# Two layers of a streaming encoder on one core: a modulation split throughout, later rows normed early, a last gate beside the first output tile, and norm steps, loads and weight splits placed elsewhere

## The chip, the cores and the metric

The kernel runs on one core of a Trainium2 chip, in one launch. A core has a matrix engine (TensorE, PE in the profile), VectorE (DVE), ScalarE (ACT), GpSimd (POOL) and the sync engine (SP), each with its own queue of instructions. The metric is the device time of one execution in microseconds (us); less is better.

## The reference, cut to what matters

Two layers run over 2048 prompt rows and 32 sample rows of width 1024. Layer 0 mixes with a gated linear recurrence (RG-LRU), layer 1 with forgetting attention (FoX). All is fp32.

```python
def _adaln(c, w, b):
    mod = jax.nn.silu(c) @ w + b                 # [., 3072], w is [1024, 3072]
    shift, scale, gate = jnp.split(mod[:, None, :], 3, axis=-1)

def layer(i, x, c):
    sh, sc, gt = _adaln(c, ada_w[i], ada_b[i])
    h = _rmsnorm(x, norm_pre[i]) * (1.0 + sc) + sh
    y = _rglru_branch(h, ...) if i == 0 else _fox_branch(h, ...)
    return x + gt * _rmsnorm(y, norm_post[i])

def _rglru_branch(h, ...):                       # width 1536, 12 blocks of 128
    xb, gate = jnp.split(h @ w_in, 2, axis=-1)
    xc = conv_b + sum(xp[:, k:k + T] * conv_w[k] for k in range(4))
    r, ig = sigmoid(xblk @ w_a + b_a), sigmoid(xblk @ w_x + b_x)
    log_a = -8 * r * softplus(-lam)
    a, u = exp(log_a), sqrt(-expm1(2 * log_a)) * (ig * xc)
    hs = scan of hs[t] = a[t] * hs[t-1] + u[t]
    return (hs * silu(gate)) @ w_out

def _fox_branch(h, ...):                         # 16 heads of 64, 512 cached rows
    q, k, v, g, fl = jnp.split(h @ w_in, ...)
    log_f = log_sigmoid(fl + b_f); cum = cumsum(log_f)
    p = softmax(q k / 8 + cum[q] - cum[k], causal)
    return ((p @ v) * silu(g)) @ w_out
```

## The kernel before

Every fp32 product is made of three fp32r matmuls: each operand is split into a high part (a copy rounded to fp32r on ScalarE or GpSimd, `hi_act` L95, `hi_pool` L98) and a low part (the difference, `lo_dve` L104 on VectorE), and hi×hi, hi×lo and lo×hi are accumulated. An instruction scheduler fixes the order on each engine at build time, from the order in which the generators below are advanced and from the pools' buffers: `get(role)` takes a buffer of a pool (h 32, w 5, raw 3, half 5, ahalf 11, c 12, wg 2) and waits for its last user. All DMAs go through the one queue of SP, in the order in which they are issued. Tile names in the profile are the pools' names, and PSUM banks are called pj, st, mx, pva and pvb.

The stages, in order of time:

- The modulation of layer 0. `ada(layer, ns, ...)` loads the 512-wide columns n of `ada_w` as 8 tiles each (L243), multiplies them (L296, 34 rows) and finishes (L258 to L276) into `shv`, `gsv` (shift and scaled norm weight) or, for n ≥ 4, the gate, stored to `gp_d`. A tile for which `whole(i)` holds is multiplied unsplit in fp32; of the first call's 32 tiles that is every third one. Beside it, `prenorm` loads the rows of x in four groups of 256 (L337), takes mean squares on ScalarE (`stats`, L346), scales on VectorE (L353), transposes on PE (L372) and applies scale and shift (L378).
- The RG-LRU blocks, twice 12 (`lru_in`, half 0 and 1): chains of 24 matmuls (L556) for x and gate, `conv`, the block before's `gates` (L569, two sigmoids L570) and `tail` (L589 to L612: Exp, Tanh, products, Sqrt, scan, store of z). The list `before` holds the gates and the tail of the block before, which are called behind the first chunk and behind `conv`. As fillers run: the rest of the modulations of both layers, x's second half, the k and v cache.
- The output tiles of layer 0: `out_tiles` makes 16 tiles of 128 rows and one of the 32 sample rows, 72 matmuls each (L725, 12 steps k of 6), with z of the next tile loaded and split half way. `end` applies the gate and the residual (L753, L754). Then `norm_tile` norms the new rows for layer 1 in steps, one behind each k of the next tile: squares, mean and power, scaling (L445), transposes and affine (L452, L453) in two steps, hi, lo and store to `hb_d`. The last gate of layer 1, `last = ada(1, (4, 5), ...)`, all unsplit, is advanced once per three k.
- Layer 1: `proj` (L962 for v, L1001 for q, k and g) for two halves of the rows, with the normed rows read back by `load_h`, merged by `merge` with the `attention` stream. That stream takes key blocks step by step: row maxima (L1147, L1150), scores (L1181, L1185), exponentials (L1187), lows (L104), products with v (L1233, L1234). Where a job isn't ready it yields None, and the projection goes on. Behind the projection come the split of w3 (`load_wout`), 7 output tiles inside the attention stream (`out_tiles`, 48 matmuls each) and 10 behind it.

`merge` alternates by credit: each advance of the projection gives the attention stream its cost in ns times 1.25, and a None sets the credit to 0.

```python
            if k == 0 and end is not None:
                nxt = end()
```

## Time and profile before

| | |
|---|---|
| median of three runs | 3038.46 us (3029.72 to 3040.52) |
| the profiled execution: its time, its span | 3031.66 us, 3029.7 us |
| mean granted clock of PE | 0.985 |
| PE busy | 2869.4 us, 95% of the span |
| VectorE, ScalarE, GpSimd busy | 61%, 48%, 41% |
| matmul instructions | 14948 |

Times in the profile are counted from the span's start. A busy share says little of what a stage is worth; the waits of PE and the tables by stretch say where time can go. The span and the time of the profiled execution differ by 2 us, which lie around the program.

### The profile page before, as it was taken

The numbers are of one execution on the slowest core, as the hardware profiler recorded it, in microseconds if no ns is written. First come the engines' busy times: TensorE is split into PE (matmuls) and PEld (weight loads), VectorE is DVE, ScalarE is ACT, GpSimd is POOL, SyncE is SP. The second block draws the span as 40 slices with busy tenths as digits, with TensorE's granted clock in tenths as the row PEclk, the third lists the DMA queues.
The fourth block names the chain that finished last, engine by engine and source line by source line (L and its number), as shares of the span: only waits on it lengthen the run. The fifth ranks groups of instructions, "written<-read, shape, count | busy, mean of one in ns | idle before, by whom it ended". The sixth has DMA issues, their size and how long they took to land.

```text
span 3029.7 us, 45098 instructions
## 1 busy us (share of the span) xinstructions
PE 2869.4 (95%) x14948; PEld 2293.8 (76%) x14948; DVE 1837.2 (61%) x3282; ACT 1465.3 (48%) x2962; POOL 1255.6 (41%) x1166
## 2 busy tenths in 40 slices
PE   6999999999999989999999999999999999989998
PEld 3777788897666677777777677887888788766776
DVE  7688777777432335646554565766776676676622
ACT  4565544556333333535354443665566556555621
POOL 5445443333222232434343332554555545455632
PEclk9999999999999999999999999999999999998999
DMA  7565675443644587676776776556555556464243
GB/s 277 197 220 199 218 270 192 151 152 127 191 135 129 161 302 254 187 247 187 222 220 210 227 222 192 147 176 154 152 155 152 165 148 176 131 164 121 82 135 96
DMA packets 407002, 548.40 MB, mean 181 GB/s; under 512 B 77096, under 2 KB 241064, under 8 KB 406768
## 3 DMA queue, kind: packets, MB, share of 16 engines
q1 hardware_dynamic: 406768, 545.50, 59.1%
q8 instruction: 119, 1.95, 0.3%
q14 instruction: 115, 0.94, 0.1%
HBM read 333.13 MB, written 212.22 MB: 180 GB/s over the span
## 4 chain that ended last, share of the span: by engine, by line
PE 38%; DMA 8%; DVE 6%; issue 5%; POOL 4%; ACT 3%; SPq 1%; POOLq 0%; DVEq 0%; ACTq 0%
PE pj L1001 13%; PE pj L962 4%; PE mx L1147 4%; PE st L1185 3%; PE st L1181 3%; PE pva L1233 3%; PE pvb L1234 3%; DVE ahalf L104 2%; DMA rc<-dn_d 1%; POOL ahalf L1210 1%; DVE mxs L1150 1%; PE pj L725 1%; DMA ahalf<-q_d 1%; POOL half L754 1%; PE mx L1376 1%
## 5 line engine op out<-in xcount | busy, mean ns | idle before, releaser
L1210 POOL TENSOR_TENSOR ahalf<-ahalf,ahalf 128x512 f32<-128x512 f32 (+2 forms) x528 | 582.5, 1103 | 418.7 <-ACT ahalf L1187 405.1
L1001 PE MATMUL pj<-h,w 128*128 128x512 f32 (+1 forms) x2304 | 585.3, 364 | 1.2 <-DVE half L104 1.2
L1187 ACT ACTIVATE ahalf<-st 128x512 fp32r<-128x512 f32 (+3 forms) x640 | 341.3, 533 | 376.0 <-PE st L1185 327.7
L104 DVE TENSOR_TENSOR ahalf<-st,ahalf 128x512 fp32r<-128x512 f32 (+3 forms) x640 | 386.9, 606 | 206.9 <-ACT st L1188 192.7
L1001 PEld LDWEIGHTS pj<-h,w 128*128 128x128 f32 x2304 | 424.5, 191 | 83.9 <-DVE half L104 1.4
L1150 DVE TENSOR_REDUCE mxs<-mx 128x1 f32<-128x512 f32 (+3 forms) x640 | 372.2, 605 | 148.0 <-PE mx L1147 84.9
L1188 ACT ACTIVATE st<-st 128x512 f32<-128x512 f32 (+3 forms) x640 | 339.8, 531 | 0.0
L1181 PE MATMUL st<-ahalf,kv 128*128 128x512 f32 (+3 forms) x640 | 244.0, 381 | 24.0 <-DVE ahalf L104 17.0
L1233 PE MATMUL pva<-ahalf,vs 128*128 128x512 f32 (+3 forms) x640 | 240.9, 388 | 10.8 <-POOL ahalf L1200 6.6
L962 PE MATMUL pj<-w,h 128*128 128x256 f32 (+3 forms) x1296 | 234.3, 288 | 12.1 <-DVE flog L977 5.4
L1185 PE MATMUL st<-ahalf,kb 96*128 96x512 f32 (+3 forms) x640 | 242.6, 386 | 1.0 <-ACT ahalf L1168 0.6
L1234 PE MATMUL pvb<-ahalf,vs 128*65 128x512 f32 (+3 forms) x640 | 228.1, 366 | 5.7 <-DVE od L1262 3.5
L1147 PE MATMUL mx<-kb,qm 96*128 96x512 f32 (+3 forms) x640 | 225.4, 384 | 7.2 <-DMA ext_d<-half 6.1
L556 PE MATMUL pj<-h,w 128*128 128x512 f32 (+1 forms) x1032 | 226.0, 369 | 0.8 <-POOL h L98 0.7
L962 PEld LDWEIGHTS pj<-w,h 128*128 128x128 f32 (+1 forms) x1296 | 192.3, 187 | 24.7 <-issue 7.5
L556 PEld LDWEIGHTS pj<-h,w 128*128 128x128 f32 x1032 | 177.3, 192 | 32.6 <-POOL h L98 0.9
L104 DVE TENSOR_TENSOR ahalf<-ahalf,ahalf 128x512 fp32r<-128x512 f32 (+2 forms) x183 | 143.9, 788 | 92.6 <-ACT ahalf L95 59.1
L104 DVE TENSOR_TENSOR w<-raw,w 128x1024 fp32r<-128x1024 f32 (+3 forms) x85 | 104.7, 1232 | 150.1 <-ACT w L95 68.5
L1001 PE MATMUL pj<-h,raw 128*128 128x272 f32 (+1 forms) x576 | 188.5, 327 | 0.0
L98 POOL TENSOR_SCALAR w<-raw 128x1024 fp32r<-128x1024 f32 (+3 forms) x68 | 76.1, 1120 | 251.5 <-DMA raw<-in_wqkg 54.2
L725 PE MATMUL pj<-h,ahalf 128*128 128x512 f32 (+1 forms) x408 | 168.2, 413 | 10.4 <-DVE ahalf L104 5.4
L1181 PEld LDWEIGHTS st<-ahalf,kv 128*128 128x128 f32 x640 | 121.7, 190 | 69.2 <-DVE ahalf L104 37.8
(325 smaller groups left out, 5615.5 us busy)
## 6 DMA issues: line engine op xcount, KB each, us to landing
wp_d<-w SPq DMA_DIRECT2D x60, 512.0 KB
vs<-v_d SPq DMA_DIRECT2D x96, 256.0 KB
kv<-k_d SPq DMA_DIRECT2D x192, 128.0 KB
ahalf<-q_d SPq DMA_DIRECT2D x192, 128.0 KB
raw<-in_w SPq DMA_DIRECT2D x44, 512.0 KB
ahalf<-in_ada_w SPq DMA_DIRECT2D x64, 256.0 KB
hb_d<-wg SPq DMA_DIRECT2D x32, 512.0 KB
v_d<-half SPq DMA_DIRECT2D x64, 256.0 KB
```

Of the source, the lines that this page charges most:

```text
L104: dve.tensor_tensor(o, i, f(h), ALU.subtract)
L556: pe.matmul(ps[:, :b - a], l, cols(r, a, b), start=i == 0, stop=i == 23)
L962: pe.matmul(ps[:m, :nw], l, r, start=c == 0, stop=c == 23)
L1001: pe.matmul(ps[:, :b - a], l, cols(r, a, b), start=c == 0, stop=c == 23)
L1147: pe.matmul(ps[:sw, :kw], u.qm[0:96, s0:s0 + sw], kb, start=True, stop=not last)
L1150: dve.tensor_reduce(u.mxs[:sw, si, c:c + 1], ps[:sw, :kw], axis=AX.X, op=ALU.max)
L1181: pe.matmul(ps[:kw, c0:nq], j.ka[k0 // 512][:, kc:kc + kw], u.qa[:, c0:nq], start=True, stop=False)
L1185: pe.matmul(ps[:kw, c0:nq], j.kb[k0 // HALF][0:96, kd:kd + kw], u.qb[0:96, c0:nq], start=False, stop=True)
L1187: act.activation(ph[:kw, c0:nq], ps[:kw, c0:nq], AF.Exp, scale=0.125)
L1188: act.activation(ps[:kw, c0:nq], ps[:kw, c0:nq], AF.Exp, scale=0.125)
L1210: pool.tensor_tensor(u.acc[:kw, c0:nq], f(ph)[:kw, c0:nq], u.acc[:kw, c0:nq], ALU.add)
L1233: pe.matmul(u.pva[:, c:nq], vs[:kw, 0:128], ph[:kw, c:nq], start=ti == 0, stop=last)
```

## The change

Nine edits, independent of each other in the code:

1. The first modulation splits all its 32 tiles; the high parts alternate between ScalarE and GpSimd. Its bias tiles move from the pool c to the pool half.
2. `prenorm` loads the groups 2 and 3 into the pool c as soon as their turn comes before the first block, takes their statistics ahead of group 1's transposes, and `lru_in` gets `fill`: while the first two chains run, it advances the norm by one step behind every three matmuls.
3. The LRU's `tail` is cut in two: Exp, Tanh and products run behind the last chunk's x chain, Sqrt, scan and store behind `conv`.
4. The last gate's tiles go into the pool w, `out_tiles` is started ahead of the last block's gates (z of tile 0 loaded and split), and the modulation advances behind every k.
5. `norm_tile` has two more empty steps ahead of its transposes.
6. `load_h` for the second 512 columns moves from the last tile's loop into the 16 V steps.
7. `LOAD_STEPS` is 18, was 10.
8. q is loaded six steps ahead of a unit's end, was four.
9. w3's raw tiles are loaded two ahead, and its split is handed out in pieces that cost 1500 ns of credit each.

```diff
-ADA_FIRST, ADA_LAST = 8, 6
+ADA_FIRST, ADA_LAST = 8, 5
-LOAD_STEPS = 10
+LOAD_STEPS = 18
...
-                    hi_pool(a, t)
+                    (hi_act if ahead > 6 and i % 2 else hi_pool)(a, t)
...
-                    x = get("xn", [w, pw])
+                    x = get("xn" if gi < 2 else "any", [w, pw])
...
-        ahead = 2
-        for gi in range(ahead):
+        for gi in range(2):
             load(gi)
-        done = 0
+        for gi in range(2):
+            stats(gi)
+        yield 0.0
+        for gi in range(2, len(groups)):
+            load(gi)
+        yield 0.0
         for gi, (t0, n, w) in enumerate(groups):
-            while done < min(gi + (1 if gi == 1 else 2), len(groups)):
-                stats(done)
-                done += 1
-            yield 0.0
+            if gi == 1:
+                stats(2)
+                stats(3)
...
         del o2
         yield
+        yield
+        yield
         for k0 in (0, 4):
...
+                if fill is not None:
+                    next(fill, None)
...
             dve.scalar_tensor_tensor(th, r, 1.0, th, ALU.add, ALU.mult)
+            s.update(a=a, th=th)
+
+        def tail2(n):
+            s = st.pop(n)
+            r, ig, sg, a, th = s["r"], s["ig"], s["sg"], s["a"], s["th"]
             act.activation(th, th, AF.Sqrt)
...
+                if ci == len(chs) - 1:
+                    before[1]()
                 ps = bank()
                 chain(ps, wgh, wgl, a, b)
...
             conv(n)
-            before[1]()
-            before = (lambda n=n: gates(n), lambda n=n: tail(n))
+            before[2]()
+            before = (lambda n=n: gates(n), lambda n=n: tail(n), lambda n=n: tail2(n))
...
                     (hi_pool if k % 2 else hi_act)(a, t[:, c])
+                    if ahead:
+                        yield 1500.0
                     lo_dve(b, t[:, c], a)
...
-            yield 0.0
+            del t, a, b, prs
+            if ahead:
+                load(k + ahead)
+            yield 1500.0 if ahead else 0.0
...
-            lds = [(max(0, late - 4), lambda: q_load(u))]
+            lds = [(max(0, late - 6), lambda: q_load(u))]
...
-        set_roles(first, "c", N_C, "any", "gp", "wout", "ap", "ab")
+        set_roles(first, "c", N_C, "any", "gp", "wout", "ap")
+        set_roles(big, "half", N_HALF, "ab")
...
-        run(ada(0, (0, 2, 1, 3), bank0, bank0, ADA_FIRST, lambda i: i % 3 == 0))
+        run(ada(0, (0, 2, 1, 3), bank0, bank0, ADA_FIRST))
...
-        blocks = lru_in(0, h, bank0, bank1, lc, rest)
+        blocks = lru_in(0, h, bank0, bank1, lc, rest, pre)
...
+        set_roles(big, "w", N_W, "aw")
+        gps = {0: None, 1: None}
+        tiles = list(range(8)) + [16] + list(range(8, 16))
+        out = out_tiles(tiles, NB, z_d, io["x"], x1_d, gps, bank0, w, post=lambda t, o2: norm_tile(t, o2, bank1))
+        next(out)
         last = ada(1, (4, 5), bpvb, bank0, ADA_LAST, lambda i: True)
-        next(last)
...
         for i in range(16 * NB):
             next(out)
-            if i % 3 == 0:
-                next(last, None)
+            next(last, None)
...
             if k < KD:
-                for g in range(2):
-                    run(load_h(h, hb_d, g, 512 * g, 512, [k]))
+                run(load_h(h, hb_d, 0, 0, 512, [k]))
         tail = run(out)
+        loads = load_h(h, hb_d, 1, 512, 512)
...
             next(tail, None)
+            next(loads, None)
         run(tail)
+        run(loads)
...
-        yield from load_wout(io["w3"], NP, w)
+        yield from load_wout(io["w3"], NP, w, 2)
```

Of what this does to the order on PE, three places follow. The first is the passage from the last RG-LRU chain to the output tiles, before the change: the last split modulation step (`scs`), then tile 0 (L725), the last gate's unsplit steps (`scf`, L296) and the last block's gates (L569).

```order
L296 MATMUL pvb_6118<-ahalf_6629,scs 34x512
L296 MATMUL pvb_6118<-ahalf_6630,scs 34x512
L725 MATMUL pj_7001<-h_6637,ahalf_6983 128x512
L725 MATMUL pj_7001<-h_6638,ahalf_6983 128x512
L296 MATMUL pvb_6845<-ahalf_6831,scf 34x512
L569 MATMUL pva_6889<-c_6791,half_6280 128x354
L569 MATMUL mx_6894<-c_6791,half_6280 128x354
L569 MATMUL mx_6899<-c_6791,half_6280 128x354
L296 MATMUL pvb_6845<-ahalf_6833,scf 34x512
L569 MATMUL pva_6889<-c_6792,half_6280 128x354
```

After the change (L754 is the tile's line, L574 the gates'):

```order
L754 MATMUL pj_7036<-h_6736,ahalf_6888 128x512
L754 MATMUL st_7037<-h_6738,ahalf_6888 128x512
L754 MATMUL pj_7036<-h_6735,ahalf_6889 128x512
L754 MATMUL st_7037<-h_6737,ahalf_6889 128x512
L296 MATMUL pvb_7060<-w_7054,scf 34x512
L574 MATMUL pva_6942<-c_6866,half_6345 128x354
L574 MATMUL mx_6947<-c_6866,half_6345 128x354
L574 MATMUL mx_6952<-c_6866,half_6345 128x354
L754 MATMUL pj_7036<-h_6902,ahalf_6892 128x512
L754 MATMUL st_7037<-h_6904,ahalf_6892 128x512
L574 MATMUL pva_6942<-c_6867,half_6345 128x354
```

Ahead of these rows stand the first three steps k of tile 0, each with a modulation step behind it: PE now finds 24 matmuls of the tile and four modulation steps ahead of the gates, where two matmuls and one step stood.

The second place is the third output tile, around the first transpose (L452) of the norm of the tile before; the weights h_66.. and h_68.. change with each step k of six matmuls. Before:

```order
L296 MATMUL pvb_7251<-ahalf_7249,scf 34x512
L725 MATMUL pj_7430<-h_6849,ahalf_7367 128x512
L725 MATMUL st_7431<-h_6851,ahalf_7367 128x512
L725 MATMUL pj_7430<-h_6850,ahalf_7367 128x512
L725 MATMUL st_7431<-h_6852,ahalf_7367 128x512
L725 MATMUL pj_7430<-h_6849,ahalf_7368 128x512
L725 MATMUL st_7431<-h_6851,ahalf_7368 128x512
L452 MATMUL mx_7481<-ident,c_7454 128x128
L725 MATMUL pj_7430<-h_6859,ahalf_7367 128x512
```

After (the transpose is L455):

```order
L754 MATMUL pj_7495<-h_6912,ahalf_7417 128x512
L754 MATMUL st_7496<-h_6914,ahalf_7417 128x512
L754 MATMUL pj_7495<-h_6922,ahalf_7416 128x512
L754 MATMUL st_7496<-h_6924,ahalf_7416 128x512
L754 MATMUL pj_7495<-h_6923,ahalf_7416 128x512
L754 MATMUL st_7496<-h_6925,ahalf_7416 128x512
L754 MATMUL pj_7495<-h_6922,ahalf_7417 128x512
L754 MATMUL st_7496<-h_6924,ahalf_7417 128x512
L455 MATMUL mx_7570<-ident,c_7518 128x128
L754 MATMUL pj_7495<-h_6932,ahalf_7416 128x512
```

The transpose moved from behind the fifth step k, 30 matmuls, to behind the seventh, 42; it is so in each tile from the third on.

The third place is where the second projection ends (L1001) and the attention steps go on (L1147 maxima, L1181 and L1185 scores, L1233 and L1234 products). Before, up to the first output tile of layer 1 (L725):

```order
L1181 MATMUL st_28503<-ahalf_28105,kv_27789 128x512
L1185 MATMUL st_28503<-ahalf_28106,kb_9698 128x512
L1234 MATMUL pvb_28294<-ahalf_28362,vs_9702 65x512
L1147 MATMUL mx_28510<-kb_9698,qm_9701 128x512
L1147 MATMUL mx_28513<-kb_9698,qm_9701 128x512
L1233 MATMUL pva_28293<-ahalf_28506,vs_9702 128x512
L1181 MATMUL st_28534<-ahalf_28105,kv_28064 128x512
L1185 MATMUL st_28534<-ahalf_28106,kb_9698 128x512
L1234 MATMUL pvb_28294<-ahalf_28389,vs_9702 65x512
L1343 MATMUL mx_28518<-identr,mx_s 32x32
L1147 MATMUL mx_28541<-kb_9699,qm_9701 128x512
L725 MATMUL pj_28491<-h_28403,w_28485 128x512
```

After, from the same attention step on (L1176 maxima, L1210 and L1214 scores, L1262 and L1263 products), no tile has begun:

```order
L1210 MATMUL st_28474<-ahalf_28122,kv_27844 128x512
L1214 MATMUL st_28474<-ahalf_28123,kb_9753 128x512
L1263 MATMUL pvb_28352<-ahalf_28422,vs_9757 65x512
L1176 MATMUL mx_28481<-kb_9753,qm_9756 128x512
L1176 MATMUL mx_28484<-kb_9753,qm_9756 128x512
L1262 MATMUL pva_28351<-ahalf_28448,vs_9757 128x512
L1372 MATMUL mx_28491<-identr,mx_s 32x32
L1176 MATMUL mx_28503<-kb_9754,qm_9756 128x512
L1176 MATMUL mx_28506<-kb_9754,qm_9756 128x512
L1178 MATMUL mx_28506<-mask_q,identr 128x128
```

The first matmul of an output tile moved from 25 rows behind the projection's last one to 122 rows behind it, from the third attention step behind the projection to the sixteenth. Before attention's last step stand 216 of the 816 matmuls of these tiles before the change and 90 after it.

## Rows read from the trace of the kernel before

**Rows 1.** The page: span; busy time of each engine.

```profile
span 3029.7 us, 45098 instructions
...
PE 2869.4 (95%) x14948; PEld 2293.8 (76%) x14948; DVE 1837.2 (61%) x3282; ACT 1465.3 (48%) x2962; POOL 1255.6 (41%) x1166
```

**Rows 2.** Windows: stretch, length, busy us per engine, clock, DMA share, GB/s.

```profile
0.00:56.00 56.00, 34.55 (x110) 11.62 (x110) 43.10 (x103) 17.07 (x38) 32.20 (x49) 0.92 0.78 269
80.00:729.00 649.00, 635.46 (x3338) 538.30 (x3337) 488.99 (x580) 346.24 (x493) 259.99 (x199) 0.99 0.58 195
729.00:776.00 47.00, 34.24 (x117) 20.43 (x116) 38.14 (x48) 25.54 (x33) 16.36 (x9) 0.82 0.49 155
776.00:1096.00 320.00, 303.93 (x1300) 214.64 (x1299) 101.73 (x197) 121.81 (x304) 78.40 (x83) 1.00 0.54 165
1096.00:1130.00 34.00, 28.11 (x201) 26.45 (x200) 8.74 (x24) 10.53 (x30) 12.85 (x26) 0.95 0.96 314
1820.00:1832.00 12.00, 5.89 (x47) 5.48 (x46) 3.63 (x7) 1.00 (x2) 0.00 (x0) 0.85 0.80 229
1832.00:2660.00 828.00, 807.79 (x4727) 674.71 (x4727) 553.96 (x1121) 472.68 (x1039) 415.40 (x366) 0.99 0.57 157
2660.00:2690.00 30.00, 24.34 (x116) 19.13 (x115) 20.59 (x35) 16.58 (x31) 16.53 (x14) 0.94 0.62 186
2690.00:2875.00 185.00, 172.61 (x799) 129.60 (x798) 132.71 (x253) 108.58 (x233) 108.55 (x98) 0.94 0.42 116
```

**Rows 3.** Windows, matmuls of L725 alone (output tiles): PE, PEld.

```profile
2880.00:3029.00 149.00, 137.13 (x593) 107.16 (x591) 0.99 0.38 116
```

**Rows 4.** Waits of PE, whole span: us in total, times, longest.

```profile
PE mx L452 <- DVE c L445: 9.3, 9, 1.2
...
PE pva L452 <- DVE c L445: 6.3, 6, 1.3
PE mx L1147 <- DMA ext_d<-half: 6.1, 1, 6.1
PE pj L725 <- DVE ahalf L104: 5.4, 1, 5.4
PE pj L962 <- DVE flog L977: 5.4, 3, 4.8
PE pj L725 <- ACT ahalf L95: 5.0, 2, 3.8
PE st L1181 <- DMA ahalf<-q_d: 4.6, 5, 1.9
PE pvb L296 <- DVE half L259: 3.7, 2, 2.3
```

**Rows 5.** Timeline of DVE: start, length, instruction; idle before it.

```profile
44.30 1.52 DVE L104 TENSOR_TENSOR c<-h,c 128x512 fp32r<-128x512 f32 x1
...
756.04 2.20 DVE L104 TENSOR_TENSOR c<-raw,c 128x1024 fp32r<-128x1024 f32 x1 [5.24 <-ACT c L95]
...
765.74 1.21 DVE L104 TENSOR_TENSOR c<-raw,c 128x1024 fp32r<-128x1024 f32 x1
```

**Rows 6.** Windows, matmuls of L296 alone (modulation): PE, PEld.

```profile
729.00:776.00 47.00, 9.33 (x16) 1.48 (x16) 0.82 0.49 155
```

**Rows 7.** Groups by line from 0 to 57 us: busy, mean ns, idle before.

```profile
L104 DVE TENSOR_TENSOR c<-h,c 128x512 fp32r<-128x512 f32 x21 | 18.7, 925 | 1.8 <-POOL c L98 1.8
```

**Rows 8.** Timeline of PE, the third chain's first matmul.

```profile
75.57 0.50 PE L556 MATMUL pj<-h,w 128*128 128x512 f32 x1 [0.70 <-POOL h L98]
```

**Rows 9.** Groups by line from 80 to 729 us: table loads ahead of Sqrt.

```profile
L594 ACT ACT_TABLE_LOAD x22 | 28.2, 1283 | 0.4
```

**Rows 10.** Waits of PE from 2660 to 2690 us.

```profile
PE st L1181 <- DVE ahalf L104: 5.6, 3, 3.2
```

**Rows 11.** Windows of 12 us, columns as in the second group.

```profile
2736.00:2748.00 12.00, 8.29 (x29) 4.61 (x29) 7.83 (x15) 7.05 (x15) 9.55 (x10) 0.94 0.56 167
2784.00:2796.00 12.00, 12.00 (x48) 9.28 (x48) 5.65 (x13) 6.21 (x16) 5.35 (x6) 0.57 0.40 121
```

More of the change, by code (lines that the diff above doesn't have):

```diff
@@ L383, in prenorm @@
                 yield 110 * n
-            if gi + ahead < len(groups):
-                load(gi + ahead)
             flags.add(("n", layer, half, gi))
@@ L656, in lru_in, with load_wout, load @@
             conv(n)
-            before[1]()
-            before = (lambda n=n: gates(n), lambda n=n: tail(n))
-        return before
-    def load_wout(src, kn, w):
+            before[2]()
+            before = (lambda n=n: gates(n), lambda n=n: tail(n), lambda n=n: tail2(n))
+        return before
+    def load_wout(src, kn, w, ahead=0):
+        raw = {}
+        def load(k):
+            if k < kn:
+                raw[k] = get("raw", [128, D])
+                sp.dma_start(raw[k], src[128 * k:128 * k + 128, :])
+        for k in range(ahead):
+            load(k)
         for k in range(kn):
-            t = get("raw", [128, D])
-            sp.dma_start(t, src[128 * k:128 * k + 128, :])
+            if not ahead:
+                load(k)
+            t = raw.pop(k)
             if k >= 8:
@@ L1658, in hybrid_kernel @@
         run(wout)
[L1659 removed]
+        gps.update({i: load_gp(0, i) for i in range(2)})
         ones_rows()
         h = new_h()
[L1662 to L1663 removed]
         for i in range(16 * NB):
             next(out)
[L1666 to L1667 removed]
+            next(last, None)
         run(last)
```

18 lines of the change are left out of this document (9 added, 9 removed).

## The prediction

> **What bounds the kernel now.** I read the page first: TensorE (PE) is busy in 2869.4 of 3029.7 us, the next engine, VectorE (DVE), in 61% of the span [rows 1]. So only two things can shorten the run much: idle time of PE, 160 us in all (3029.7 − 2869.4), and stretches at a clock under 1.00, where a busy PE does less. The second view is a table of stretches [rows 2]; the reader is to see in it that the idle time is not even. The matmul stages are almost full (80 to 729 us: 13.5 idle of 649). Idle are the start (21.5 of 56), the passage from the RG-LRU blocks to the output tiles (729 to 776: 12.8 of 47, at a clock of 0.82), the tiles (776 to 1096: 16.1 of 320), the passage to the attention layer (1096 to 1130: 5.9), 6.1 of 12 at 1820, and the end of attention (2660 to 2875: 18.1 at 0.94). Third, the waits of each such stretch say what ended them. As a yardstick I take the pitch of the output tiles' matmuls where nothing interrupts them: 137.13 us for 593, or 0.231 us each [rows 3].
>
> **The change part by part.** The sum is made against the profiled execution, 3031.66 us for a span of 3029.7.
>
> Norm steps further apart. PE waits 15 times for the DVE scaling of L445 that its transposes read, 9.3 + 6.3 = 15.6 us, each at most 1.3 [rows 4]: nearly all that is idle in the tiles' stretch. The order moves the transposes of a tile from behind 30 of its 72 matmuls to behind 42. Those 12 matmuls take 12 × 0.231 = 2.8 us, more than twice the longest wait, and the instructions that the transposes wait for stay where they are. What is late next is the tile's evacuation, split and store, 2.8 us later in a 20 us tile (320/16), which nobody awaits before the tile is over. I take −14; at the least −8, if the evacuations now meet the next tile's split of z on ScalarE; at the most −15.6.
>
> The last gate beside the first output tile. Now tile 0 ends at about 776 us, 46 us after the last chain, and its own work is 72 × 0.231 = 16.7. In that stretch PE waits 5.4 us for the low part of z, 5.0 for the high one and up to 2.3 for a gate's finish [rows 4]. After, z of tile 0 is loaded and split ahead of the last gates, PE has the tile's first four steps and four modulation steps to do before the gates, and all 16 steps of the modulation stand in the first two tiles, where 7 did in the first. The limit is then the w2 rows with k ≥ 8: their low parts stand on DVE at 756.0 to 767 [rows 5], among the products and scan of the last block. Tile 0 needs the last of them for its last step, so it ends about 768.5 if DVE keeps its times, and about 763 if the z splits that left that stretch pull it forward. That is 7 to 12 us, and PE will have done some 5 more modulation steps by then, of 9.33/8 = 1.2 us each (seven whole steps and a split one stand in that stretch [rows 6]). The ceiling is all idle time and the clock's loss, 12.8 + 0.18 × 34.24 = 19. I take −13; bounds −4 (only the z waits that the gates don't hide) and −19.
>
> More load steps. At 1820 us PE waits 6.1 us for the bias rows ext_d [rows 4]. The attention stream now lets the projection make 18 steps instead of 10 before it computes its first maxima. A step is three matmuls, so eight are 8 × 3 × 0.231 = 5.5 us of PE work in place of the wait: −5.5; bounds 0 (the work is only moved within a stretch that is full anyway) and −7 (the clock of 0.85 there recovers as well). q loads two steps earlier are for the waits on q_d, 4.6 us in five [rows 4]; they hold slots of the ahalf pool longer, so −1, between +3 and −4.6.
>
> The later h loads in the 16 V steps. They move behind the last tile's stores on the SP queue, so that the V tiles 4 and 5 wait for DMA, and the last tile's transposes come later. The stretch holds 5.9 us of idle time now, 5.4 of it waits for flog, which stay [rows 2, 4]. I take +1, between −4 and +5.
>
> First modulation all split, prenorm early. Eleven weight tiles lose their fp32 matmuls and gain split ones, which PE has room for; DVE gets 11 more lows of 0.925 us by the mean [rows 7], 10 us. The last low starts at 44.30 and ends at 45.8 [rows 5], late in the 56 us before the first chain, so these are not free; but DVE stood idle 12.9 of the first 56 us [rows 2], and some of the lows fall there. The biases move to a pool whose slots are free only after the rates of the LRU, so the weight loads behind the fourth queue behind a bias load that waits for DVE, and there the awaited instruction stands behind the low of the first weight tile: a tile has to land and be split, its low alone 0.925 us, before the fifth is fetched. That is 2 to 4 us of loads lost, an estimate of mine, ahead of a chain whose last low is late by DVE's queue and not by its load. Against it the later rows' transposes leave the gap between the second and third chain, where the last wait of PE is 0.70 us [rows 8]. I take +1; bounds −4 (DVE's waits go and the idle 12.9 us absorb all) and +8 (most of the 10 us on the path).
>
> The LRU tail in two parts. Ten more table loads of 1.28 us [rows 9] are 13 us on ScalarE, which is busy 346 of 649 us in that stage [rows 2]; PE fills it, so 0 (±4).
>
> Split of w3 spread out, tiles later. After the projection ends, attention has 78 steps left in either order. Before, 216 of the output tiles' 816 matmuls stand among them, after, 90; 126 × 0.231 = 29 us move behind attention's end. Whether that is lost depends on how far attention alone shrinks. The 185 us from 2690 hold 81 steps, 210 tile matmuls and 172.61 us of busy PE, so a step's own PE work is (172.61 − 210 × 0.231)/81 = 1.53 us, and a step takes 2.28 [rows 2, 3]. DVE, the next, has 132.71/81 = 1.64 with its share of the tiles. With 90 tile matmuls inside, PE has 81 × 1.53 + 21 = 145 us of work; at the same busy share of 93% that is 156, plus 29 behind is 185: no change. And the bunched waits of 2660 to 2690 (5.6 us [rows 10]) may go, but the splits now fall among steps with less cover. The granted clock of these 185 us is 0.94 now, with one fall to 0.57 over 12 us at 2784, not long after 3.7 us of 12 were idle at 2736 [rows 11]; by the mean the price above stands, and by the fall it is rival 2. The Trainium skill (TensorE: Matmul & The Clock Gate, "A second HAM failure mode: psum-queue depth-cycling") tells of a kernel whose PE idled briefly between groups of matmuls so often that its clock went to and fro; by that rule attention without filler loses its clock, as rival 2 has it, and the sum would go by that rival's price. I take 0. Bounds: −16 (145 + 29 against 185, and the 5.6), and +29 (the pace of 2.28 stays, and the removed work only bares waits).
>
> Sum: −14 − 13 − 5.5 − 1 + 1 + 1 + 0 + 0 = −31.5, so 3031.66 − 31.5 = 3000. The profiled execution lies 6.8 us under the median 3038.46 of the runs shown, and near their lowest, 3029.72; against the median the sum gives 3007. I keep 3000.
>
> **Rivals.**
> 1. Attention alone keeps its pace: +29 in the last part, 3029. For it: between 2690 and 2875 PE waits for DVE, ScalarE and POOL in turn, and fillers hide this. Against it: DVE, the next, has 132.71 us there [rows 2], tiles included, under the 156.
> 2. Slower: attention alone, in the 16 steps before the first tile and between sparse ones, loses the clock. Its place is 2690 to 2845, its price follows from rows: at the 0.57 of those 12 us throughout, the work of 145 us at 0.94 takes 239, +29 is 268 against 185: +83, 3083. It decides from a clock c at which 145 × 0.94/c + 29 = 185 + 31.5, c = 0.73; for over 0.5% slower, 0.67. Against it: the stretch has 0.94 as a mean now, and attention with projection runs at 0.99 [rows 2].
> 3. The passage and the norm steps don't gain: waits of the transposes reappear on the evacuation, or the gate's finish stays the end of tile 0; 14 + 13 less 4 stays, 3023.
> 4. Faster: attention contracts to its PE work, the passage reaches its ceiling: −16 − 6, 2978.
>
> **How the numbers follow.** Runs of this kernel scatter by 10.8 us, so about 0.5%, 15 us, is what can be told from no change. Chances: the sum 0.70; rival 1 0.09; rival 2 0.05; rival 3 0.08; rival 4 0.08. The likeliest gives 3000, with a range of its own of 2984 to 3020 from the bounds of its terms. The range 2978 to 3026 takes in rivals 3 and 4 and leaves out rivals 1 and 2 and a little of the tails. Faster by over 15 us: the sum, rival 4 and a part of rival 3, 0.81; within: rivals 1 and 3 and the sum's upper tail, 0.14; slower 0.05.
>
> **What would show it.** Right: no waits of the transposes on the scaling in the tiles; tile 0 over by some 13 us earlier counted from the last chain; no wait for ext_d over 1 us; attention's stretch shorter by about what the ten to thirty us of tiles behind it cost. Wrong: a start whose first chain begins after 62 us, PE idle or a clock under 0.75 in the steps between the projection's end and the tiles, or waits for the later halves of h in the V steps over 5 us.

## The result, and the profile after

The changed kernel takes 3058.05 us (median of five runs, 3055.63 to 3069.28), the kernel before in the same runs 3030.37 (3025.44 to 3040.52): 1.0091 times as long, with a 95% interval of 1.0062 to 1.012. The forecast was 3000 us with a range of 2978 to 3026. The profiled execution took 3055.63 us. One execution, in the run with ten load steps, took 4939.83 us at a granted clock of 0.79 and is left out of that run's median.

The page of the changed kernel, its span and busy times, answers to [rows 1]: PE has the same instructions and 5 us more of busy time in a span that is 24.2 us longer, so most of the loss, 19 us, is idle time of PE, and the rest a lower clock.

```profile
span 3053.9 us, 45125 instructions
...
PE 2874.4 (94%) x14948; PEld 2299.4 (75%) x14948; DVE 1804.8 (59%) x3293; ACT 1488.0 (49%) x2988; POOL 1273.5 (42%) x1161
```

Where it lies is seen when the program is cut at the same events in both traces. The events are read from the timelines of PE: the first matmul of the first RG-LRU chain, the end of the last chain, the first v projection, the first projection of q, k and g, the end of the last one, the start of attention's last score step, and the end of PE's last matmul.

| stretch, us | before | after | difference | forecast of the difference |
|---|---|---|---|---|
| up to the first chain | 56.5 | 67.9 | +11.4 | +1 |
| first to last chain (24 blocks) | 673.0 | 717.6 | +44.6 | 0 |
| to the first v projection (gates, tiles) | 366.2 | 329.5 | −36.7 | −27 |
| v projections, up to the first q, k or g | 34.1 | 41.7 | +7.6 | +1 |
| projections with attention | 1569.6 | 1556.6 | −13.0 | −6.5 |
| attention behind the projections | 177.2 | 152.5 | −24.7 | 0 for this row and the next |
| the tiles behind attention | 145.0 | 179.9 | +34.9 | |

The same stretches as windows of the changed kernel (columns as in [rows 2]; the last one runs on to the span's end, 8 us behind PE's last matmul):

```profile
0.00:68.00 68.00, 32.91 (x115) 13.02 (x115) 53.10 (x123) 31.95 (x72) 32.52 (x46) 0.84 0.78 269
68.00:785.00 717.00, 674.82 (x3436) 564.82 (x3435) 472.35 (x624) 383.09 (x540) 294.37 (x224) 0.96 0.54 182
785.00:1115.00 330.00, 328.65 (x1407) 232.78 (x1406) 127.09 (x230) 135.15 (x322) 91.57 (x91) 1.00 0.57 176
1115.00:1157.00 42.00, 32.06 (x202) 29.03 (x202) 8.78 (x24) 10.46 (x31) 12.89 (x26) 0.84 0.91 299
1157.00:2713.00 1556.00, 1495.75 (x8433) 1226.31 (x8432) 979.95 (x1985) 792.86 (x1734) 685.27 (x635) 0.99 0.66 187
2713.00:2866.00 153.00, 136.26 (x630) 97.49 (x629) 115.85 (x227) 97.60 (x207) 98.00 (x87) 0.96 0.43 106
2866.00:3053.90 187.90, 173.92 (x736) 136.00 (x736) 47.64 (x84) 36.94 (x85) 58.92 (x56) 0.96 0.38 119
```

The second row is the surprise. Of its 717 us PE is idle 42.2, and the granted clock is 0.96. The same stretch before has 15.0 us of idle time at 0.99:

```profile
57.00:730.00 673.00, 658.01 (x3434) 554.49 (x3432) 505.88 (x617) 363.67 (x535) 272.86 (x223) 0.99 0.58 198
```

The third row is nearly full: the tiles have 1.4 us idle where they had 16.1, and the passage ahead of them none to speak of.

The waits of PE over the whole span (us in total, times, longest), of which those of L455 and of L296 with pvb answer to [rows 4]:

```profile
PE st L1210 <- DVE ahalf L104: 30.9, 35, 7.4
...
PE pj L296 <- DVE c L104: 10.2, 15, 3.7
...
PE pj L991 <- DMA h<-hb_d: 7.6, 6, 2.5
...
PE pva L574 <- DVE c L104: 6.8, 5, 2.7
...
PE st L559 <- DVE wg L104: 4.9, 3, 2.7
...
PE pvb L296 <- DVE half L259: 4.4, 3, 3.5
...
PE mx L1176 <- DMA qm<-q_d: 3.2, 1, 3.2
...
PE mx L455 <- DVE c L446: 2.2, 2, 1.1
```

The transposes' wait for the scaling is down from 15.6 us to 2.2 in this view, the waits of tile 0 for z and the one for ext_d are gone. Waits for VectorE's lows (L104) have grown everywhere: in the start (L296, 3.0 before, 10.2 now), for the weights of the chains (L559, 1.2 and 4.9) and in front of the scores (L1210, 17.0 and 30.9). Those in the gates (L574) are new, and the waits for h in the v projections went from 2.6 to 7.6.

Within the second stretch alone, all waits of PE that VectorE ended come to 30.2 us (4.4 before). The low of conv's result is only 7.3 of them; the others are for the finish of a modulation (L259, L260), lows of weights and products with the gate:

```profile
PE pva L574 <- DVE c L104: 6.8, 5, 2.7
PE st L269 <- DVE half L260: 6.5, 2, 3.8
PE st L559 <- DVE wg L104: 4.9, 3, 2.7
PE pvb L296 <- DVE half L259: 4.4, 3, 3.5
...
PE st L559 <- DVE c L654: 2.4, 1, 2.4
```

### The profile page after: what moved, and what is told of

It is laid out like the page before. It is cut to its first block, busy times and chain, and to the rows that moved or that the text cites. A ratio compares the mean times of both kernels' runs of the same rounds, so it can differ in the third digit from the quotient of the medians.

```text
span 3053.9 us, 45125 instructions
## 1 busy us (share of the span) xinstructions
PE 2874.4 (94%) x14948; PEld 2299.4 (75%) x14948; DVE 1804.8 (59%) x3293; ACT 1488.0 (49%) x2988; POOL 1273.5 (42%) x1161
## 5 line engine op out<-in xcount | busy, mean ns | idle before, releaser
L1030 PE MATMUL pj<-h,w 128*128 128x512 f32 (+1 forms) x2304 | 592.5, 364 | 0.4 <-DVE half L104 0.4
L104 DVE TENSOR_TENSOR ahalf<-st,ahalf 128x512 fp32r<-128x512 f32 (+3 forms) x640 | 386.7, 605 | 209.7 <-ACT st L1217 182.4
L1210 PE MATMUL st<-ahalf,kv 128*128 128x512 f32 (+3 forms) x640 | 245.9, 384 | 32.2 <-DVE ahalf L104 30.9
L1262 PE MATMUL pva<-ahalf,vs 128*128 128x512 f32 (+3 forms) x640 | 241.6, 388 | 12.7 <-ACT ahalf L1216 7.5
L1214 PE MATMUL st<-ahalf,kb 96*128 96x512 f32 (+3 forms) x640 | 243.3, 386 | 4.7 <-ACT ahalf L1197 4.3
L104 DVE TENSOR_TENSOR w<-raw,w 128x1024 fp32r<-128x1024 f32 (+3 forms) x85 | 108.7, 1278 | 216.6 <-ACT w L95 88.3
L559 PE MATMUL pj<-h,w 128*128 128x512 f32 (+1 forms) x1056 | 231.8, 372 | 1.5 <-DVE c L654 1.0
L1176 PE MATMUL mx<-kb,qm 96*128 96x512 f32 (+3 forms) x640 | 225.4, 383 | 7.5 <-DMA qm<-q_d 3.2
L1263 PE MATMUL pvb<-ahalf,vs 128*65 128x512 f32 (+3 forms) x640 | 228.3, 365 | 3.0 <-DVE od L1291 2.1
L991 PEld LDWEIGHTS pj<-w,h 128*128 128x128 f32 (+1 forms) x1296 | 191.8, 189 | 24.2 <-DMA h<-hb_d 9.7
L559 PEld LDWEIGHTS pj<-h,w 128*128 128x128 f32 x1056 | 182.8, 193 | 35.0 <-DVE c L654 1.5
L559 PE MATMUL st<-h,wg 128*128 128x512 f32 (+1 forms) x792 | 182.7, 385 | 9.4 <-DVE wg L104 4.9
L1210 PEld LDWEIGHTS st<-ahalf,kv 128*128 128x128 f32 x640 | 121.4, 190 | 75.0 <-DVE ahalf L104 54.2
L104 DVE TENSOR_TENSOR ahalf<-ahalf,ahalf 128x512 fp32r<-128x512 f32 (+2 forms) x183 | 137.0, 750 | 61.2 <-ACT ahalf L95 31.5
```

The lines of the kernel that those rows point to most:

```text
L104: dve.tensor_tensor(o, i, f(h), ALU.subtract)
L559: pe.matmul(ps[:, :b - a], l, cols(r, a, b), start=i == 0, stop=i == 23)
L991: pe.matmul(ps[:m, :nw], l, r, start=c == 0, stop=c == 23)
L1030: pe.matmul(ps[:, :b - a], l, cols(r, a, b), start=c == 0, stop=c == 23)
L1210: pe.matmul(ps[:kw, c0:nq], j.ka[k0 // 512][:, kc:kc + kw], u.qa[:, c0:nq], start=True, stop=False)
L1214: pe.matmul(ps[:kw, c0:nq], j.kb[k0 // HALF][0:96, kd:kd + kw], u.qb[0:96, c0:nq], start=False, stop=True)
```

## The experiments

In all of them "first to last chain" is the second stretch of the table. Four further builds that left the split tail alone (the runs of 13 buffers, of the modulation, of w3 and v loads, and of the biases) took 709.9 to 714.5 us there, against 717.6, so up to 8 us of a difference between two profiles may be scatter.

**The tail whole again.** All of the tail behind conv, in the changed kernel.

```diff
-                if ci == len(chs) - 1:
-                    before[1]()
...
-            before[2]()
-            before = (lambda n=n: gates(n), lambda n=n: tail(n), lambda n=n: tail2(n))
+            before[1]()
+            before = (lambda n=n: gates(n), lambda n=n: tail(n))
```

> The changed kernel with the LRU tail whole again, behind conv, as before; all other edits stay. The time from the first RG-LRU chain to the last is 669.8 us before the change and 714.4 after it. Theory 1 (the tail's first half stands ahead of conv on VectorE and stops its queue): the stretch falls to 670 +- 8, the time from 3056 to 3012. Rival (the later rows in pool c, early, or the fill of the first chains cost it): the stretch stays at 705 to 720, the time at 3050 to 3060.

677.0 us, and 3017.28 us, 0.9961 of before (0.9946 to 0.9977): with this one edit taken back the changed kernel is the faster one. Between these two profiles the split tail carries 40.6 of the 44.6 us, and of the waits that VectorE ended there 8.6 us are left.

**The tail split alone**, in the kernel before.

> The kernel before with the tail cut in two and nothing else. Theory 1: the stretch from first to last chain grows from 670 to 705 to 720, the time from 3030 to 3065 to 3080. Rival (later rows in pool c and the fill): the stretch stays at 670 +- 5, the time at 3030 +- 6.

707.1 us and 3057.27 us, 1.01 (1.0085 to 1.0115): the edit does it by itself, with 34.1 us here; the time rose less than expected. The waits of PE that VectorE ended are 27.6 us, as in the changed kernel. The passage behind the last chain is 6 us shorter in this run (366.2 to 359.9).

**What of the tail does it** was less easy. In the seventh block of the changed kernel, VectorE's timeline (start, length, instruction; in brackets the idle time before and what ended it) shows the taps of conv (L584), and ahead of them, between them and behind them the tail of the block before: its product (L598), the product with Sqrt (L605) and the scan (L607), 1.6 + 2.1 + 2.3 us. The low part of conv's result (L104, c) comes last, at 288.41. ScalarE had run conv's first operation at 271.05.

```profile
273.93 1.62 DVE L598 SCALAR_TENSOR_TENSOR c<-c,c 128x1024 f32<-128x1024 f32 x1 [1.79 <-POOL c L596]
...
277.00 2.82 DVE L584 SCALAR_TENSOR_TENSOR c<-c,prm,c 128x1024 f32<-128x1024 f32 x2
279.75 2.05 DVE L605 TENSOR_TENSOR c<-c,c 128x1024 f32<-128x1024 f32 x1
...
282.33 1.21 DVE L104 TENSOR_TENSOR wg<-raw,wg 128x1024 fp32r<-128x1024 f32 x1
...
284.06 1.27 DVE L584 SCALAR_TENSOR_TENSOR c<-c,prm,c 128x1024 f32<-128x1024 f32 x1
285.26 2.28 DVE L607 TENSOR_TENSOR_SCAN c<-c,c 128x1024 f32<-128x1024 f32 x1
288.41 1.22 DVE L104 TENSOR_TENSOR c<-c,c 128x1024 fp32r<-128x1024 f32 x1 [0.88 <-POOL c L98]
```

PE meanwhile waits for the low of the next weights (wg at 282.33) and for the low of conv:

```profile
283.60 5.39 PE L559 MATMUL st<-h,wg 128*128 128x512 f32 x22 [1.46 <-DVE wg L104]
...
289.69 0.73 PE L574 MATMUL mx<-c,half 128*128 128x512 f32 x2 [0.47 <-DVE c L104]
```

With the whole tail the same block reads so: all three taps at 257.92 (ScalarE's operation was at 256.64), the low at 266.58, and behind it the tail.

```profile
257.92 3.92 DVE L584 SCALAR_TENSOR_TENSOR c<-c,prm,c 128x1024 f32<-128x1024 f32 x3 [0.18 <-ACT c L582]
...
266.58 2.91 DVE L104 TENSOR_TENSOR c<-c,c 128x1024 fp32r<-128x1024 f32 x1
...
270.22 1.21 DVE L598 SCALAR_TENSOR_TENSOR c<-c,c 128x1024 f32<-128x1024 f32 x1
...
272.55 1.23 DVE L600 TENSOR_TENSOR c<-c,c 128x1024 f32<-128x1024 f32 x1 [1.13 <-ACT c L599]
273.81 2.29 DVE L602 TENSOR_TENSOR_SCAN c<-c,c 128x1024 f32<-128x1024 f32 x1
```

So the low comes 17.4 us behind conv's first operation with the split and 9.9 without. Over the 24 blocks, from the timelines of ScalarE and VectorE, the mean is 12.1 us with the split (longest 18.3) and 9.0 before (12.4). The time from the end of the last x evacuation to conv's first operation is the same, 0.1 us in both. The two halves differ. In eleven of the first twelve blocks the product and the one with Sqrt stand between conv's first operation and the low, as here, and the low of these twelve comes 14.3 us behind in place of 9.9. In the last twelve the product stands ahead of conv, and what is left in front of the low is mostly the tail's last product (L617): 9.9 in place of 8.1. But the order in time is no proof: Exp and Tanh, GpSimd's products and two buffers of pool c stand ahead of conv as well. Seven runs separate them.

*The product behind conv*: `dve.scalar_tensor_tensor(th, ...)` moved from the first half to the second.

> The changed kernel with one instruction of the tail moved: VectorE's product with the tanh stands in the second half, behind conv; Exp, Tanh and GpSimd's products stay ahead of it, and so do the two buffers of pool c that the first half takes. Theory 1 (order on VectorE): the stretch from first to last chain falls from 714 to 670 to 690, the time to 3012 to 3030. Rival (the two buffers of pool c held through conv, or GpSimd's queue with the products ahead of conv's high part): the stretch stays at 700 to 720, the time at 3045 to 3060.

712.2 us, 3049.92 us. I read this at first as a strike against VectorE's order. It was not: in VectorE's timeline the product still stands ahead of conv's low in every block that follows another, and the low came 11.8 us behind conv's first operation. The edit did not do what I meant it to do.

*The two buffers early*: the whole tail behind conv, its two tiles of pool c taken where the split takes them.

> The changed kernel with the whole tail behind conv again, but its two buffers of pool c taken where the split takes them, behind the last x chain, ahead of conv's three. No instruction stands earlier than in the run with the whole tail (first to last chain 677.0 us, time 3017). Theory A (pool c is short: conv's tiles wait for buffers): the stretch is 700 to 718 and the time 3040 to 3058. Theory B (the queues: instructions of the tail ahead of conv stop ScalarE, GpSimd and VectorE): the stretch stays at 677 +- 6, the time at 3017 +- 8.

678.0 us and 3018.46 us: holding the buffers costs nothing.

*13 buffers*: `N_C = 13`.

> The changed kernel with 13 buffers in pool c in place of 12, the most that fits; the split tail stays. Theory A (pool c is short): first to last chain falls from 717.6 by 15 us or more, the time to 3040 or less. Theory B (queues): 717.6 +- 8, the time 3056 +- 8.

711.4 us and 3049.59 us: within the scatter of the split's builds. One more buffer does not help, and with the run before the pool is not it.

*GpSimd's products behind conv too*: only Exp and Tanh stay in the first half.

> The changed kernel with Exp and Tanh ahead of conv, and GpSimd's two products and VectorE's one behind it, so that GpSimd's rounding of conv's result for the gates no longer stands behind 4.9 us of products. Theory B in the form that GpSimd's queue does it: first to last chain falls from 717.6 to 675 to 690, the time to 3015 to 3030. In the form that ScalarE's queue does it (Exp, Tanh and their table load ahead of the gate chain's sigmoid), or by theory A (two buffers held): it stays at 700 to 718, the time at 3040 to 3058.

712.9 us and 3058.25 us, low 11.8 us behind: VectorE's product and what follows it again stand ahead of the low, as in the run with the product moved.

*Copies in conv's path*: the whole tail, and in each block

```diff
+            for _ in range(4):
+                act.activation(xb[:, 3:3 + cw], xb[:, 3:3 + cw], AF.Copy)
             act.activation(xc, xb[:, 0:cw], AF.Identity, scale=prm[:, n, 0:1], bias=prm[:, n, 4:5])
```

> The changed kernel with the whole tail (first to last chain 677.0 us), and in each block four copies of a tile onto itself on ScalarE ahead of conv's first operation, some 4.5 us, about what Exp, Tanh and their table loads take (1.17 + 1.15 + 2 x 1.28). The result is as before. Theory S (ScalarE's queue: what delays conv's input by some 5 us makes the gates' operands and the weights' lows behind it late): the stretch grows to 700 to 720, the time from 3017 to 3040 to 3060. Rival (a delay of conv alone is covered; the loss needs Exp between the gates' sigmoids or VectorE waiting for the products): 677 to 687, 3017 to 3027.

749.9 us, more than expected, and 3089.91 us. The copies in the groups by line, from 80 to 800 us:

```profile
L582 ACT ACTIVATE c<-c 128x1024 f32<-128x1024 f32 (+1 forms) x92 | 98.6, 1072 | 55.5 <-DVE convc L660 39.6 <-DVE convs L663 14.6
```

They did more than delay conv by their own length: ScalarE waited 55.5 us in front of them for VectorE's copies out of the same tile (L660, L663), so that conv's first operation came 8.5 us behind the evacuation, and its other work stood behind them as well: PE waited 16.1 us in the stretch for the norm's affine steps (L420).

*As many copies off the path*, of an unused tile:

> The changed kernel with the whole tail (first to last chain 677.0 us) and four copies of an unused tile onto itself on ScalarE per block, issued behind conv's first operations, where nothing waits for them; e12 had as many in conv's path and took 749.9. Theory P (the place counts: conv's input is late): 677 to 695, time 3017 to 3035. Rival L (ScalarE's load counts, wherever it stands): 715 to 750, time 3055 to 3090.

676.1 us and 3018.77 us. 96 copies ran, but all of them before 236 us: 29 ahead of the first chain and 67 in the first 165 us of the stretch. The groups by line:

```profile
L587 ACT ACTIVATE junk<-junk 128x1024 f32<-128x1024 f32 x96 | 101.7, 1060 | 2.0 <-DVE junk L1619 1.0
```

Some 71 us more of ScalarE's work in the first quarter of the stretch cost nothing, and some 99 in front of conv cost 73. So work on ScalarE is not dear in itself; its place is. That only the way to conv's low is dear is not shown by these two runs, since in the first of them other results of ScalarE were late too.

*VectorE's tail held behind conv's low*: the split stays, and the product's summand 1 is taken from an element of the low, times 0 plus 1.

```diff
-            dve.scalar_tensor_tensor(th, r, 1.0, th, ALU.add, ALU.mult)
...
+                dve.tensor_scalar(one, f(st[n + 1]["xl"])[:, 0:1], 0.0, 1.0, ALU.mult, ALU.add)
+            dve.scalar_tensor_tensor(th, r, one, th, ALU.add, ALU.mult)
             act.activation(th, th, AF.Sqrt)
```

> The changed kernel with the split tail, but VectorE's product with the tanh takes its summand 1 from an element of conv's low part (times 0 plus 1, the same value), so that it and all that follows it (Sqrt, product, scan) can't stand ahead of conv on VectorE. Exp, Tanh and GpSimd's products stay ahead of conv. Theory V (VectorE's order): from conv's first operation to its low 9 to 10 us in the mean, first to last chain 673 to 690, time 3014 to 3030. Rival (ScalarE and GpSimd ahead of conv): 12 us, 705 to 718, 3045 to 3058.

676.8 us, and 3015.1 us (0.9962, 0.9946 to 0.9978); the low stands 9.0 us behind conv's first operation. Exp, Tanh and GpSimd's products still come ahead of conv's low, so they are cleared. The window of the chains in this run:

```profile
68.00:745.00 677.00, 661.22 (x3441) 556.25 (x3441) 485.52 (x639) 392.79 (x549) 265.51 (x223) 0.99 0.57 193
```

And the table loads in front of ScalarE's sigmoids of the gate chains, in the same window:

```profile
L657 ACT ACT_TABLE_LOAD x45 | 57.7, 1283 | 12.5 <-PE st L559 11.8
```

PE is idle 15.8 us of 677 at a clock of 0.99, against 42.2 of 717 at 0.96. The stretch has 91 table loads, 24 more than before the change and 10 more than the changed kernel, and they cost nothing. This settles the cause: VectorE's part of the tail, let in front of conv's low and of the other results that PE waits for. The Sqrt on ScalarE, which lies between two of VectorE's products, went back with them; no run separates it.

**The norm of the first rows as before.**

> The changed kernel with the norm of the first half's rows as before: groups 2 and 3 loaded late into the old pool, statistics as before, no fill in the first two chains. Theory 1: the stretch from first to last chain stays near 714 (+- 8), the first chain comes some 5 us earlier than 67.9 since ScalarE's squares of the later rows no longer stand ahead of group 1, and the time is 3050 +- 6. Rival (later rows and fill): the stretch falls to 670 to 680 and the time to 3010 to 3018.

The first chain comes at 64.4, 3.5 us earlier, and the chains take 705.4, so the early later rows cost about 3.5 us at the start and some 5 to 12 more in the chains beside the split (with the whole tail 676.1 to 678.0, where the builds without this edit take 670.4 to 673.0); the time is 3045.97 us. Neither expectation held alone: the 45 us are not in this edit, but it is not free.

**The first modulation as before**, and then only **its biases back in pool c**.

> The changed kernel with the first modulation as before: every third tile unsplit, biases in pool c, all high parts on GpSimd. Theory: the split and the queued loads cost 6 us up to the last modulation matmul (52.2 against 45.9), and the squares of the later rows the rest; so the first chain comes at 60 to 63 in place of 67.9, and the time is 3049 +- 5. Rival (the squares and the full pool c make all of it): the first chain stays at 66 to 68 and the time at 3056 +- 4.

> The changed kernel with the biases of the first modulation back in pool c, so that no weight load queues behind them; all 32 tiles stay split. Undoing both gave a first chain at 59.5 in place of 67.9. Theory: the queued loads make most of it, the first chain comes at 60 to 63. Rival: the eleven more lows on VectorE make it, 65 to 68.

Without both the first chain comes at 59.5 (3044.92 us), with the biases back and the split kept at 65.7 (3051.37 us), so that the expectation that the queued loads make most of it missed. The queue of weight loads behind the biases is worth 2.2 us, the eleven splits, with the high parts that went to ScalarE, 6.2, and with the 3.5 of the later rows the 11.4 us are accounted for (2.2 + 6.2 + 3.5 = 11.9). The timeline of PE in the changed kernel shows two of the three: the last modulation matmuls at 52.17, and 4.66 us of waiting for L381 at 65.28, while ScalarE squares later rows, eight times from 59.77 to 64.67.

```profile
52.17 1.78 PE L296 MATMUL pj<-c,scs 128*34 128x512 f32 x3 [0.38 <-DVE c L104]
57.08 0.58 PE L269 MATMUL st<-ident,half 2*128 2x2 f32 x4 [3.12 <-DVE half L260]
...
65.28 1.14 PE L375 MATMUL mx<-ident,ahalf 128*128 128x128 f32 x4 [4.66 <-ACT ahalf L381]
...
67.93 0.78 PE L559 MATMUL pj<-h,w 128*128 128x512 f32 x1
```

**The norm steps alone**, in the kernel before.

> The kernel before with the two empty steps of the norm and nothing else. By the prediction's step the tiles' stretch, from the last chain's end to the first v projection, falls from 366.2 by 14, to 352, and the time by 14, to 3014. Rival (the waits move to the evacuation): 361 to 368, 3025 to 3030.

The tiles' stretch takes 348.1 us, 18.1 less, and the v projections 38.6, 4.5 more: −13.6 in sum. The time is 3006.85 us, 0.9937 of before (0.9921 to 0.9953). What the later transposes give up is in the waits of the v projections, where flog was 5.4 us in sum [rows 4]:

```profile
PE pj L964 <- DVE flog L979: 6.7, 3, 6.2
PE pj L964 <- DMA h<-hb_d: 1.7, 1, 1.7
```

**w3 and the v loads as before**, in the changed kernel.

> The changed kernel with w3 split in one go and the later h loads inside the last tile's loop, as before; the two places lie 1500 us apart and are read apart. Theory: from the first v projection to the second projection stage 41.7 falls to 33 to 37; attention behind the projection and the rest, 152.5 + 179.9 = 332.4, fall to 318 to 325; the time falls from 3056 to 3036 to 3045. Rival for the v part (it comes from the tiles' earlier end): 40 to 43. Rival for w3 (the attention steps are slower for another reason): 330 to 335.

The v stretch falls from 41.7 to 38.4, so the later h loads cost 3.3 us there and the norm steps the other 4.5. Flog is waited for instead of h:

```profile
PE pj L991 <- DVE flog L1006: 7.0, 3, 6.1
...
PE pj L991 <- DMA h<-hb_d: 0.8, 1, 0.8
```

Attention behind the projections and the rest take 177.8 + 148.5 = 326.3 in place of 332.4, and the time is 3042.85; both stretches stay a little above what was expected. The 6 us are what the stretch scatters by among twelve builds with equal code there (328.6 to 334.7), and the run of the gains below, with w3 as before, took 331.8; so the spread split of w3 costs between nothing and some 6 us. Neither run shows a gain.

**The gains only**, **norm steps and gate only**, and **ten load steps**, from the kernel before.

> The kernel before with only the parts that gained: norm steps apart, last gate beside the first tile, 18 load steps, q loads earlier; first modulation, prenorm, tail, v loads and w3 as before. If the stages add up: 56.5 + 673 + 330 + 35 + 1558 + 322 + 8 us behind PE's last matmul = 2982, time 2980 to 2992, 1.3% below before. If the gains of the tiles come at a price in a neighbouring stage, 2995 or more.

> The kernel before with two of the nine edits: the norm steps apart and the last gate beside the first tile. Without the 18 load steps and the q loads at six. Theory (those two gain nothing on balance: the wait for the bias rows becomes waits for the lows of q): the second stretch of projection and attention stays within 1553 to 1570, attention behind it at 177 + 145, the time 2985 to 2996, not above the 2995 of the run with them. Rival (they gain their 6 us): 3000 to 3004.

> As the run with the gains only, 2995.3, but with 10 load steps; q loads stay at six steps ahead. If the q loads cost what the load steps gain: the wait for ext_d of 6 us is back and the waits for the lows in front of the scores stay at 20 us; 2998 to 3003. If the load steps moved the waits: the waits for the lows fall to 10 us as before and the time to 2987 to 2994.

Times, in the order of the expectations: 2995.27 us (0.9906 of before, 0.9888 to 0.9924), 2995.35 (0.9907, 0.9887 to 0.9927) and 2999.96 (0.9915, 0.9896 to 0.9934). With two of the nine edits the time is as low as with four. The intervals are some 6 us to either side, so a gain or a loss of up to some 8 us by the load steps and earlier q loads is not excluded by the times. In the waits of PE the ext_d wait and the lows in front of the scores change places. With the norm steps and the gate only:

```profile
PE st L1201 <- DVE ahalf L104: 17.0, 18, 2.5
...
PE mx L1167 <- DMA ext_d<-half: 5.4, 1, 5.4
```

With the load steps and the q loads too:

```profile
PE st L1201 <- DVE ahalf L104: 34.8, 34, 5.8
...
PE mx L1167 <- DMA qm<-q_d: 3.6, 1, 3.6
```

The third run, with 10 load steps and q at six, has neither wait large, 13 us for the lows, and is no faster: its time fits the first expectation, its waits fit neither.

## Why the prediction was wrong

**The LRU tail: the step that failed.** The prediction had it as "Ten more table loads of 1.28 us [rows 9] are 13 us on ScalarE, which is busy 346 of 649 us in that stage [rows 2]; PE fills it, so 0 (±4)". The stretch grew by 44.6 us in the profile; taking the edit back gives 40.6 of them, and the edit alone costs 34.1. I priced the added work and not the moved one, and I took the busy share of the engine whose loads are added. That part of the step holds: the changed kernel has 14 more table loads in the stretch, and the run with the tail held back has 24 more and no loss. It is not the question. On VectorE, 75% busy there (488.99 of 649 [rows 2]), the last block's tail went in front of results that PE waits for: the low for the gates came 3.1 us later in the mean, and with it the lows of weights and the finish of modulations. PE lost 27 us of idle time (42.2 less 15.0), 26 of them in waits that VectorE ended, and the rest, some 17 in this profile, to the clock. That last part varies: in the run of the tail split alone it is 10 us beside 24 of idle time. The prediction argued from PE's order alone, and none of its rivals named this. A wait of VectorE says it at once: the product with the tanh waits 43.4 us for GpSimd at its new place, ahead of conv's low, and had waited 11.3 us at its old one, behind it. Before, from 80 to 729 us:

```profile
DVE c L593 <- POOL c L591: 11.3, 5, 3.3
```

After, from 80 to 782 us:

```profile
DVE c L598 <- POOL c L596: 43.4, 14, 5.3
```

**The first modulation and the later rows**: +1 was forecast, with a bound of +8; +11.4 came, and the first chain began at 67.9 us, beyond the 62 that the prediction had named as a sign of being wrong. The two halves were named (lows on VectorE, loads behind the biases), but the squares of the later rows in ScalarE's queue, ahead of group 1's affine steps, were not priced at all: 3.5 us. Of the eleven lows it was said that "some of the lows fall there", in VectorE's idle time; the splits delayed the first chain by 6.2 us, where their lows are 10 us of work. The 2 to 4 us of lost loads, an estimate, measured 2.2.

**The norm steps**: mechanism and size were right, −14 forecast, −18.1 + 4.5 = −13.6 measured alone. That the last tile's transposes would come later had been put under the h loads.

**The last gate**: −13 forecast; 348.1 to 335.2 us with it added to the norm steps, −12.9. Tile 0 is over 32.7 us behind the last chain in the changed kernel and was over 46.3 us behind it, 13.6 less, as forecast. Where the further 6 us in the changed kernel come from stays open: with the tail whole again the stretch is 330.8, so it is not the split.

**The v loads**: +1 forecast; +3.3 by the loads, within its bounds. The waits for h in the changed kernel, 7.6 us, are the second of the named signs of being wrong.

**The load steps and q loads**: −6.5 forecast. The wait for ext_d did go, but no gain shows in the time: 2995.27 with them, 2995.35 without. The −13 of the table is in part scatter, since 1569.6 us is the longest of the four profiles without the two edits (1559.3 to 1569.6); the 14 with both took 1553.6 to 1565.0. Behind the projections it is the other way: 319.5 to 322.2 without them, 326.3 and 331.8 with them and w3 as before. The two stretches together take 1881.2 to 1891.8 without the edits and 1883.0 and 1891.3 with them, so what the first gains the second seems to give back. The step that did not hold is taking a wait in one execution for a gain: where two streams are merged, PE's next work is moved, and the waits for the lows grew from 17.0 to 30.9 us in the changed kernel.

**w3**: 0 forecast, between −16 and +29; +10.2 with the load steps' share in it, nothing to 6 by itself. Attention alone took 152.5 us, near the 156 worked out (for three steps more), with a clock of 0.96, so the rival with the lost clock did not hold. The estimate took the busy share of 93% over; it was 89% (135.80 of 152.50), 4 us more of idle time than before. The tiles behind took 34.9 us more and not 29, at a clock of 0.97 where it was 1.00 and with 2.7 us more idle. The bunched waits before the projections' end did not go either: one low is waited for 7.4 us up to 2692, which is in the table's row of the projections, and behind their end one exponential 6.0. In the waits from 2653 to 2866 us:

```profile
PE st L1210 <- DVE ahalf L104: 11.5, 10, 7.4
PE pva L1262 <- ACT ahalf L1216: 7.5, 4, 6.0
```

In attention without filler the granted clock fell to 0.50, the lower level of 1.2 GHz, twice for 6.8 us, once behind 4.6 us of idle time in 5.3, and came back each time; with the fillers before it fell three times, and the mean was 0.94. As windows of the changed kernel:

```profile
2748.00:2753.30 5.30, 0.71 (x3) 0.18 (x2) 0.81 (x2) 0.23 (x1) 0.00 (x0) 1.00 0.77 174
2753.30:2760.10 6.80, 5.44 (x13) 4.25 (x14) 4.87 (x8) 3.88 (x7) 4.01 (x5) 0.50 0.23 64
```

The Trainium skill (TensorE: Matmul & The Clock Gate, "A second HAM failure mode: psum-queue depth-cycling"), weighed there, tells of such a clock that goes to and fro; the trace agrees in that. Rival 2's price did not come: the mean stayed at 0.96.

In the chains, where PE stopped for 1 to 4 us at a time, the mean fell to 0.96 from 0.99 in the changed kernel's profile; in three others with the split tail and 39 to 45 us of idle time there it was 0.98.

## What to carry to other kernels

A part of a chain that is made ready earlier is not free because its engine has time: with a scheduler, everything behind it becomes ready earlier too, and may go ahead of what the critical engine waits for on a third engine; so print the order of every engine on the path from a bound engine's output to its next input, not only that of the bound engine. Price a move by how late it makes the next operand, and look for slack on that path by putting idle work into it and beside it, and by reading in the trace where that work ran and what it waited for. When a statement moved in the source does not move on the engine, a data dependency can hold it. A wait that a single profile shows once in a merged stretch is worth its length only if a run without it says so.

## What the runs showed that was not expected

The blocks grew by about half of the delay of conv's low: with the copies the low came 6.7 us later in the mean (15.7 from the evacuation's end against 9.1), and the blocks took 3.0 us more each; with the split 3.1 us later, and 1.7 more. This is a ratio of means and no law. By halves the split cost 22.0 us in the blocks up to the twelfth conv, where the low was 4.4 us later, and 22.6 in the rest, where it was 1.8 later (24.1 and 10.1 in the run of the split alone); other results of VectorE were late too. So little slack was there, although PE is 98% busy before the change and each block takes 28 us.

The eleven more split tiles, with their high parts on ScalarE too, moved the first chain by 6.2 us in a stretch in which VectorE is 78% busy (53.10 of 68 us).
